# Scores of 64-feature heads taken over half of the partitions, with even and odd heads in two PSUM banks

## The chip, the core and the metric

The kernel runs on one core of one Trainium2 chip. The metric is the device time of one execution in microseconds (us). Before the change the median of three runs is 1797.05 us (1796.57 to 1798.23). In the profile, PE is TensorE's multiplying part and PEld its loading of weights (the stationary operand), DVE is VectorE, ACT ScalarE, POOL GpSimd, and SP the engine that issues most DMAs.

## The reference, cut to what matters

Two blocks work on one sequence of 256 tokens with 1024 features. The first block has two layers, each with three branches, and two of them are attention with heads of 64 features; the second block has a sparse attention of 8 heads of 64 features, whose keys are chosen by an index score of 4 heads of 64 features.

```python
# first block, forgetting branch ("c"): 16 heads, per block of 128 queries
sc = jnp.einsum('bqhd,bkhd->bhqk', q[:, start:end], k[:, :end]) * scale
sc = sc + cum[:, :, start:end, None] - cum[:, :, None, :end]
probs = jax.nn.softmax(jnp.where(causal, sc, -inf), axis=-1)
# first block, sliding window branch ("b"): 16 query heads on 4 key heads, with a sink
scores = jnp.einsum('bnqkgd,bnskd->bnkgqs', qb, kb) * (HEAD_DIM ** -0.5)
probs = softmax(concatenate([where(mask, scores, -inf), sink]))[..., :-1]
# second block, sparse attention: index scores of 4 heads, then 8 heads over the chosen keys
sc = jnp.einsum('bqhd,bsd->bqhs', qib, kif) * (IDX_DIM ** -0.5)
iscore = jnp.einsum('bqh,bqhs->bqs', wib, relu(sc))
s = jnp.einsum('bqhd,bqkd->bqhk', qb, ks) * (DSA_HEAD_DIM ** -0.5)
```

The second block ends in a mixture of 32 experts (MoE), whose weights are most of what the kernel reads.

## The kernel before

**Layout.** Queries and keys are kept with features along the 128 partitions, so two heads of 64 features share a tile: the even head in partitions 0 to 63, the odd one in 64 to 127. A product of one head must leave the other out. The kernel before keeps the keys twice for that: `kz[c][0]` has the even heads' keys and zeros in the lower half, `kz[c][1]` the odd heads' keys and zeros in the upper half (lines 463, 464, 471 to 474 in branch c; 616 to 618, 636, 637 in branch b; 1131, 1132, 1140 to 1142 in the second block). So each score product runs over all 128 partitions, and the zeros cancel the other head.

**One group of heads** (`attn_heads`, line 337): the scores of 4 heads (128 keys) or 2 heads (256 keys) go into one PSUM bank `sc`, of which there are two; then DVE takes the maximum (349), ACT the exponentials with their sums (356), PE turns them round (365), ACT copies them out (367) and PE multiplies with the values into `pv` (370). In branch c every head has two products into the bank: queries by keys in float32, and a row of the decay sums `negsel_r` by `Rs` in float32r over all partitions (496). In branch b there is only the first, with one mask product for the whole bank. In the sparse attention (`dsa`) each head has its own mask product (1216).

**A float32 product** is recorded as two matmuls with a weight load each; a float32r product as one.

**Order of work.** Steps are written in a list per layer, and a scheduler orders the instructions of each engine when the kernel is built; between the steps of attention it puts the products of projections (`proj`), which are most of PE's work. PE takes its instructions in that order. The experts at the end (lines 1550, 1572) use weights of 64 columns for two experts side by side, one in columns 0 to 63 of the array, one in columns 64 to 127; the experts' other products use the full array.

The lines in question, of branch c:

```python
def scores(h, o, first):
    mm(o, qc[g][:, h // 2, t * 128:t * 128 + 128], kz[g][h % 2][:, h // 2, :nS], first, False)
    mm(o, negsel_r[:, 32 + 8 * g + h:33 + 8 * g + h].to_broadcast([128, 128]), Rs[:, :nS], False, False)
```

## Time and profile before

| what | value |
|---|---|
| median of the runs | 1797.05 us |
| the profiled execution | 1801.36 us, its span 1799.6 us |
| PE busy | 1688.6 us (94%) |
| DVE busy | 1025.9 us (57%) |
| ACT busy | 708.2 us (39%) |
| POOL busy | 318.4 us (18%) |
| chain that ended last | PE 70%, DMA 13%, DVE 11% |

The profiled execution took 4.3 us more than the median; 1.8 us of it lie outside the span. The two layers of the first block run until about 960 us, the second block's mixing until about 1320 us, and the experts to the end. A matmul's record lasts longer than the array is taken by it, since matmuls are pipelined: what a matmul costs in a dense row of them is the distance from its start to the next one's start.

### The profile page before, as it was taken

The numbers are of one execution on the slowest core, as the hardware profiler recorded it, in microseconds if no ns is written. First come the engines' busy times: TensorE is split into PE (matmuls) and PEld (weight loads), VectorE is DVE, ScalarE is ACT, GpSimd is POOL, SyncE is SP. The second block draws the span as 40 slices with busy tenths as digits, with TensorE's granted clock in tenths as the row PEclk, the third lists the DMA queues.
The fourth block names the chain that finished last, engine by engine and source line by source line (L and its number), as shares of the span: only waits on it lengthen the run. The fifth ranks groups of instructions, "written<-read, shape, count | busy, mean of one in ns | idle before, by whom it ended". The sixth has DMA issues, their size and how long they took to land.

```text
span 1799.6 us, 24178 instructions
## 1 busy us (share of the span) xinstructions
PE 1688.6 (94%) x9005; PEld 1266.1 (70%) x9005; DVE 1025.9 (57%) x1659; ACT 708.2 (39%) x1345; POOL 318.4 (18%) x247
## 2 busy tenths in 40 slices
PE   7999999999999999999998998876879999999998
PEld 6899888888798999888877876765644444434342
DVE  6656656666673568675669899799631212212121
ACT  4455555644444656565546552421411010100000
POOL 0111106220102101321024343365100000000000
PEclk9999999999999999999999998987989999999999
DMA  8654445455566534453664633223699999999997
GB/s 261 188 142 137 140 145 144 148 166 164 164 174 178 171 111 141 135 164 102 197 190 149 180 106 111 66 70 107 196 378 369 410 409 408 409 409 409 409 409 297
DMA packets 186104, 389.65 MB, mean 217 GB/s; under 512 B 28736, under 2 KB 66816, under 8 KB 185984
## 3 DMA queue, kind: packets, MB, share of 16 engines
q1 hardware_dynamic: 185984, 388.08, 63.3%
q8 instruction: 72, 1.18, 0.3%
q14 instruction: 48, 0.39, 0.1%
HBM read 386.98 MB, written 1.05 MB: 216 GB/s over the span
## 4 chain that ended last, share of the span: by engine, by line
PE 70%; DMA 13%; DVE 11%; issue 2%; POOL 2%; ACT 1%; SPq 0%; DVEq 0%; POOLq 0%; ACTq 0%
PE proj L149 45%; PE proj L1550 7%; PE sc L149 5%; PE pv L149 4%; PE sc L1572 4%; DMA whi<-in_w_up_dram 2%; DMA Tlo<-in_w_up_dram 2%; DVE wlo L217 2%; PE tp L1509 1%; PE tp L365 1%; PE tp L286 1%; DMA wlo<-in_w_up_dram 1%; DMA wx<-in_w_up_dram 1%; DMA wraw<-in_w_down_dram 1%; DVE u L935 1%
## 5 line engine op out<-in xcount | busy, mean ns | idle before, releaser
L216 ACT CAST whi<-wraw 128x1024 fp32r<-128x1024 f32 x336 | 351.8, 1051 | 319.0 <-PE proj L149 263.1
L217 DVE TENSOR_TENSOR wlo<-wraw,whi 128x1024 fp32r<-128x1024 f32 (+1 forms) x287 | 376.7, 1316 | 172.0 <-PE proj L149 119.2
L149 PE MATMUL proj<-wlo,Thi 128*128 128x512 f32 (+1 forms) x1056 | 419.4, 397 | 6.2 <-DVE wlo L217 6.2
L149 PE MATMUL proj<-whi,Thi 128*128 128x512 f32 (+1 forms) x1056 | 419.4, 399 | 2.3 <-ACT P L988 1.0
L149 PE MATMUL proj<-whi,Tlo 128*128 128x512 f32 (+1 forms) x1056 | 415.7, 396 | 2.4 <-DVE Tlo L288 2.4
L149 PEld LDWEIGHTS proj<-wlo,Thi 128*128 128x128 f32 x1056 | 201.3, 191 | 48.3 <-DVE wlo L217 8.0
L149 PEld LDWEIGHTS proj<-whi,Thi 128*128 128x128 f32 x1056 | 201.4, 191 | 44.6 <-DVE u L1273 1.9
L149 PEld LDWEIGHTS proj<-whi,Tlo 128*128 128x128 f32 x1056 | 200.9, 190 | 43.1 <-DVE Tlo L288 2.9
L217 POOL TENSOR_TENSOR wlo<-wraw,whi 128x1024 fp32r<-128x1024 f32 (+1 forms) x49 | 125.4, 2559 | 434.4 <-PE proj L149 332.4
L149 PE MATMUL proj<-Thi,whi 128*128 128x256 f32 x576 | 165.2, 291 | 6.0 <-DVE u L468 3.0
L149 PE MATMUL proj<-Thi,wlo 128*128 128x256 f32 x576 | 165.8, 289 | 3.6 <-DVE wlo L217 3.6
L149 PE MATMUL proj<-Tlo,whi 128*128 128x256 f32 x576 | 164.8, 290 | 0.1
L1554 DVE SCALAR_TENSOR_TENSOR th<-th,cg,proj 128x512 f32<-128x512 f32 x16 | 12.0, 747 | 214.1 <-PE proj L1550 212.0
L149 PEld LDWEIGHTS proj<-Thi,whi 128*128 128x128 f32 x576 | 112.5, 197 | 7.8 <-DVE u L468 3.2
L149 PEld LDWEIGHTS proj<-Thi,wlo 128*128 128x128 f32 x576 | 113.5, 197 | 4.0 <-DVE wlo L217 3.8
L149 PEld LDWEIGHTS proj<-Tlo,whi 128*128 128x128 f32 x576 | 112.6, 197 | 0.4 <-DVE Tlo L959 0.3
L149 PE MATMUL sc<-u 128*128 128x256 f32 (+1 forms) x416 | 101.0, 359 | 11.8 <-DVE u L930 11.8
L1553 ACT ACTIVATE th<-proj,cg 128x512 f32<-128x512 f32 x16 | 11.0, 687 | 192.4 <-PE proj L1550 192.4
L149 PEld LDWEIGHTS sc<-u 128*128 128x128 f32 x416 | 70.6, 198 | 20.0 <-issue 11.9
L1576 DVE TENSOR_TENSOR u<-sc,u 128x512 fp32r<-128x512 f32 x32 | 22.0, 692 | 109.5 <-ACT u L1575 90.4
L356 ACT ACTIVATE P<-sc,nm 128x256 f32<-128x256 f32 (+1 forms) x152 | 63.7, 432 | 36.2 <-DVE nm L349 22.1
L1575 ACT CAST u<-sc 128x512 fp32r<-128x512 f32 x32 | 18.6, 585 | 136.1 <-PE sc L1572 122.0
(464 smaller groups left out, 2489.1 us busy)
## 6 DMA issues: line engine op xcount, KB each, us to landing
wraw<-in_w_in_dram SPq DMA_DIRECT2D x236, 512.0 KB, 3.8
wraw<-in_w_proj_dram SPq DMA_DIRECT2D x48, 512.0 KB, 4.3
u<-in_w_up_dram SPq DMA_DIRECT2D x25, 512.0 KB, 10.2
wraw<-in_w_out_dram SPq DMA_DIRECT2D x24, 512.0 KB, 4.4
u<-in_w_gate_dram SPq DMA_DIRECT2D x24, 512.0 KB, 10.2
wraw<-in_w_up_dram SPq DMA_DIRECT2D x21, 512.0 KB, 10.2
whi<-in_w_down_dram SPq DMA_DIRECT2D x21, 512.0 KB, 10.2
u<-in_w_down_dram SPq DMA_DIRECT2D x21, 512.0 KB, 10.1
```

What stands on the lines that cost most here:

```text
L149: T.matmul(o, l, r, start=start, stop=stop)
L216: S.copy(hi[:, :, :n], raw[:, :, :n])
L217: (G if share[0] and scount[0] % share[0] == 0 else V).tensor_sub(lo[:, :, :n], raw[:, :, :n], hi[:, :, :n].bitcast(F32))
L286: T.transpose(ps[:, b, :], src[:, b * 128:(b + 1) * 128], ident)
L356: S.activation(P[:, i * nS:(i + 1) * nS], scv[:, i, :], AF.Exp, bias=nm[:, i:i + 1], accum_out=l_out[:, i:i + 1])
L365: T.transpose(tp[:, j, :], P[:, j * 128:(j + 1) * 128], ident)
L935: V.tensor_tensor_scan(m[:, 256:512], rb, hi, 0.0, op0=OP.mult, op1=OP.add)
L1509: pin(T.matmul(tp[:, k, :], src[t][:, k0 + k, :], ohv[:, t], start=n == 0, stop=n == 3))
L1550: pin(T.matmul(ps[r], xk, w[:, 512 * j:512 * j + 512], start=k == 0, stop=k == 7))
L1572: pin(T.matmul(po[c][r], hT[:, k, r], w[:, 512 * c:512 * c + 512], start=k == 0, stop=k == 3))
L1575: S.copy(yh[:, c], po[c])
L1576: V.tensor_sub(yl[:, c], po[c], yh[:, c].bitcast(F32))
```

## The change

A score product now takes only the 64 partitions of its head, of the queries and of the keys (`half_of`). Keys are kept once, so the second tile, its zeros (POOL) and one of the two copies (DVE) fall away, and ACT's copy covers all 128 partitions. `attn_heads` takes two groups of heads at once, the even heads and the odd heads, each with a bank `sc` of its own; the products alternate between the two, and what follows runs for the even group first and then the odd one. In `dsa` the mask product is one for each bank; the index scores (`select`) put even and odd heads in two banks as well. The memory branch calls with one group and computes as before. In branch c the product with `negsel_r` still follows each head's product.

```diff
-        sc = psum.tile([128, 512], F32, name="sc", bufs=2)
-        scv = sc[:, :nh * nS].rearrange("p (h s) -> p h s", h=nh)
-        for i, h in enumerate(heads):
-            scores(h, scv[:, i, :], i == 0)
-        if masks is not None:
-            masks(scv)
...
+        sc = [psum.tile([128, 512], F32, name="sc", bufs=2) for _ in groups]
+        scv = [v[:, :nh * nS].rearrange("p (h s) -> p h s", h=nh) for v in sc]
+        for i in range(nh):
+            for v, h in zip(scv, hs):
+                scores(h[i], v[:, i, :], i == 0)
+        for v, g, heads in zip(scv, groups, hs):
+            if masks is not None:
+                masks(v)
...
+    def by_halves(nh):
+        return [[slice(h0 + j, h0 + 2 * nh, 2) for j in range(2)] for h0 in range(0, 8, 2 * nh)]
+    def half_of(h):
+        return slice(64 * (h % 2), 64 * (h % 2) + 64)
...
-                S.copy(kz[c][0][0:64, b, :], ps[0:64, :])
-                V.tensor_copy(kz[c][1][64:128, b, :], ps[64:128, :])
...
-            for j in range(2):
-                G.memset(kz[c][j][64 * (1 - j):64 * (1 - j) + 64], 0.0)
-            proj_fm(xT, W, OFF1["ck"] + 512 * c, 512, ev_k(c))
+            k = kz[c] = unit().rearrange("p (h s) -> p h s", h=4)
+            proj_fm(xT, W, OFF1["ck"] + 512 * c, 512, lambda b, ps: S.copy(k[:, b, :], ps))
...
-                mm(o, qc[g][:, h // 2, t * 128:t * 128 + 128], kz[g][h % 2][:, h // 2, :nS], first, False)
+                p = half_of(h)
+                mm(o, qc[g][p, h // 2, t * 128:t * 128 + 128], kz[g][p, h // 2, :nS], first, False)
                 mm(o, negsel_r[:, 32 + 8 * g + h:33 + 8 * g + h].to_broadcast([128, 128]), Rs[:, :nS], False, False)
...
-            S.copy(Q["kT"][0][0:64, :, tt], tp[0:64])
-            V.tensor_copy(Q["kT"][1][64:128, :, tt], tp[64:128])
+            S.copy(Q["kT"][:, :, tt], tp)
...
-                mm(o, qT[g][:, h // 2, t * 128:t * 128 + 128], kT[h % 2][:, 2 * g + h // 4, :nS], first, False)
+                p = half_of(h)
+                mm(o, qT[g][p, h // 2, t * 128:t * 128 + 128], kT[p, 2 * g + h // 4, :nS], first, False)
...
-            G.memset(kT, 0.0)
...
-                for j in range(2):
-                    V.tensor_copy(kT[0:64, 2 * j, tt], tp[0:64, 2 + j, :])
-                    V.tensor_copy(kT[64:128, 2 * j + 1, tt], tp[64:128, 2 + j, :])
+                V.tensor_copy(kT[:, 0:2, tt], tp[:, 2:4, :])
...
+            ps = [psum.tile([128, 512], F32, name="sc", bufs=2) for _ in range(2)]
             for p in range(2):
...
+                    mm(ps[a][:, 256 * p:256 * p + 256], iT[half_of(a), p, t * 128:t * 128 + 128],
+                       kT[half_of(a), 1, :], True, True)
...
-                mm(o, qT[:, h // 2, t * 128:t * 128 + 128], kT[:, h % 2, :], True, False)
-                mm(o, ident_r, selm[t], False, True)
+                mm(o, qT[half_of(h), h // 2, t * 128:t * 128 + 128], kT[half_of(h), 0, :], first, False)
+            def masks(o):
+                mm(o, ident_r, selm[t][:, None, :].to_broadcast([128, 2, 256]), False, True)
```

Since the scheduler orders anew, three places on PE show what stands in a row. A name is the bank written, then what streams through the array and what is loaded as weights; numbers tell buffers apart.

PE in branch c, layer 0, the first block of queries, before: in bank `sc_1169` and then `sc_1197`, products of odd heads (keys `u_817`) and even heads (`u_816`) with the decay product between them.

```order
L149 MATMUL sc_1169<-u_817,u_687 128x128
L149 MATMUL sc_1169<-Rs_229,negsel_r_87 128x128
L149 MATMUL sc_1169<-mask_r_89,ident_r_85 128x512
L149 MATMUL sc_1197<-u_816,u_687 128x128
L149 MATMUL sc_1197<-Rs_229,negsel_r_87 128x128
L149 MATMUL sc_1197<-u_817,u_687 128x128
```

The same place in the changed kernel, where `sc_1155` takes even heads and `sc_1156` odd ones.

```order
L149 MATMUL proj_1088<-Tlo_98,whi_1121 128x256
L149 MATMUL sc_1155<-u_816,u_687 128x128
L149 MATMUL sc_1155<-Rs_229,negsel_r_87 128x128
L149 MATMUL sc_1156<-u_816,u_687 128x128
L149 MATMUL sc_1156<-Rs_229,negsel_r_87 128x128
```

Between any two products over half of the partitions stands a product over all of them; all 64 score products of branch c in the two layers stand alone like this, or have a full product of another kind beside them.

PE in branch b, layer 0, the first block of queries, before: four heads in one bank, the mask, and the next bank.

```order
L149 MATMUL sc_3057<-u_2774,u_2773 128x128
L149 MATMUL sc_3057<-u_2775,u_2773 128x128
L149 MATMUL sc_3057<-mask_r_89,ident_r_85 128x512
L149 MATMUL sc_3086<-u_2774,u_2773 128x128
L149 MATMUL sc_3086<-u_2775,u_2773 128x128
```

The same place in the changed kernel: the last two of eight products that alternate between the halves, and then both masks.

```order
L149 MATMUL sc_3038<-u_2760,u_2759 128x128
L149 MATMUL sc_3039<-u_2760,u_2759 128x128
L149 MATMUL sc_3038<-mask_r_89,ident_r_85 128x512
L149 MATMUL sc_3039<-mask_r_89,ident_r_85 128x512
L149 MATMUL proj_3293<-whi_3271,Thi_95 128x512
```

Here eight half products stand in a row, even and odd by turns, ahead of the masks of both banks.

PE in the sparse attention of the second block, before: two heads of one bank, each with its mask.

```order
L149 MATMUL proj_10809<-whi_10804,Thi_9153 128x512
L149 MATMUL proj_10809<-wlo_10805,Thi_9153 128x512
L149 MATMUL sc_10594<-u_9586,u_9938 128x256
L149 MATMUL sc_10594<-selm_9936,ident_r_85 128x256
L149 MATMUL sc_10594<-u_9586,u_9938 128x256
```

The same place in the changed kernel: two even heads together, one mask, and projections again; the odd heads' bank follows 23 rows later.

```order
L149 MATMUL proj_10755<-whi_10751,Tlo_9116 128x512
L149 MATMUL sc_10549<-u_9548,u_9893 128x256 x2
L149 MATMUL sc_10549<-selm_9891,ident_r_85 128x512
L149 MATMUL proj_10756<-whi_10751,Thi_9115 128x512
L149 MATMUL proj_10756<-wlo_10752,Thi_9115 128x512
```

The scheduler has parted the two banks here, so that two products of the same half stand together and none of the other half beside them.

## Rows read from the trace of the kernel before

**Rows 1.** Head of the page: span; chain that ended last, by engine.
```profile
span 1799.6 us, 24178 instructions
...
PE 70%; DMA 13%; DVE 11%; issue 2%; POOL 2%; ACT 1%; SPq 0%; DVEq 0%; POOLq 0%; ACTq 0%
```

**Rows 2.** Windows: stretch, length, busy time by engine, PEclk granted, DMA share, GB/s.
```profile
100.00:200.00 100.00, 100.00 (x722) 94.32 (x721) 66.20 (x99) 60.83 (x128) 13.77 (x11) 1.00 0.48 135
300.00:400.00 100.00, 100.00 (x527) 85.60 (x526) 67.41 (x115) 58.68 (x138) 26.16 (x18) 1.00 0.50 152
600.00:700.00 100.00, 100.00 (x672) 91.78 (x671) 67.51 (x107) 59.37 (x125) 2.57 (x3) 1.00 0.49 140
...
1100.00:1240.00 140.00, 112.29 (x493) 91.28 (x492) 127.00 (x181) 39.10 (x78) 71.05 (x53) 0.85 0.22 69
```

**Rows 3.** Timeline of PE in branch c: start, length, instruction (two stretches).
```profile
118.54 0.44 PE L149 MATMUL sc<-u 128*128 128x128 f32 x2
...
118.87 0.44 PE L149 MATMUL sc<-u 128*128 128x128 f32 x2
...
200.63 0.59 PE L149 MATMUL sc<-u 128*128 128x256 f32 x2
...
201.18 0.28 PE L149 MATMUL sc<-mask_r,ident_r 128*128 128x256 f32 x1
```

**Rows 4.** Timeline of PE in branch b: banks of four heads, and of two.
```profile
305.86 1.05 PE L149 MATMUL sc<-u 128*128 128x128 f32 x8
...
306.99 1.05 PE L149 MATMUL sc<-u 128*128 128x128 f32 x8
...
343.73 1.03 PE L149 MATMUL sc<-u 128*128 128x256 f32 x4
...
344.83 0.40 PE L149 MATMUL proj<-whi,Thi 128*128 128x512 f32 x1
```

**Rows 5.** Timeline of PE in the experts: full array, then weights of 64 columns.
```profile
1381.78 0.63 PE L1509 MATMUL tp<-oh,u 128*128 128x256 f32 x4
...
1382.34 0.64 PE L1572 MATMUL sc<-we,hT 128*64 128x512 f32 x1
...
1382.35 0.64 PE L1572 MATMUL sc<-u,hT 128*64 128x512 f32 x1
...
1382.82 0.59 PE L1572 MATMUL sc<-we,hT 128*64 128x512 f32 x1
...
1383.25 0.59 PE L1572 MATMUL sc<-we,hT 128*64 128x512 f32 x1
```

**Rows 6.** Timeline of PE and PEld in the experts: 64 columns, then full array.
```profile
1455.34 0.59 PE L1550 MATMUL proj<-we,u 128*64 128x512 f32 x1
...
1455.86 0.19 PEld L1586 LDWEIGHTS pv<-u,ohT 128*128 128x128 f32 x1 [0.81 <-issue]
1455.87 0.50 PE L1586 MATMUL pv<-u,ohT 128*128 128x512 f32 x1
...
1456.20 0.39 PE L1587 MATMUL pv<-u,ohT 128*128 128x512 f32 x1
...
1456.43 0.40 PE L1586 MATMUL pv<-u,ohT 128*128 128x512 f32 x1
```

**Rows 7.** By source line: copies and zeros of the keys; shortest, median, longest in ns.
```profile
L464 DVE COPY u<-proj x16: 427/428/429, 87.7 to 554.5; 64x256 f32<-64x256 f32 x16
L637 DVE COPY u<-tp x4: 694/694/695, 299.0 to 777.9; 64x512 f32<-64x512 f32 x4
L473 POOL MEMSET u<- x8: 944/946/952, 74.2 to 491.6; 64x1024 f32 x8
L618 POOL MEMSET u<- x4: 944/948/950, 256.5 to 728.6; 64x1024 f32 x4
```

**Rows 8.** Waits of PE: who waited for whom, us in total, times, longest.
```profile
PE pv L149 <- ACT PT L367: 0.9, 1, 0.9
```

**Rows 9.** Costliest groups of the page: the exponentials of all heads.
```profile
L356 ACT ACTIVATE P<-sc,nm 128x256 f32<-128x256 f32 (+1 forms) x152 | 63.7, 432 | 36.2 <-DVE nm L349 22.1
```

More of the change, by code (lines that the diff above doesn't have):

```diff
@@ L334, in run_steps, with attn_heads @@
             steps[name](*(int(v) for v in arg))
[L337 removed]
+    def attn_heads(groups, scores, vsrc, pv, pcol, nS, lsum, sink=None, masks=None):
         nb = nS // 128
[L341 to L370 removed]
@@ new lines, in attn_heads @@
+        hs = [list(range(g.start, g.stop, g.step or 1)) for g in groups]
+        nh = len(hs[0])
+        sc = [psum.tile([128, 512], F32, name="sc", bufs=2) for _ in groups]
[6 more added lines that the diff above has]
+                masks(v)
+            nm = wtile([128, 8], F32, name="nm", bufs=4)
+            V.tensor_reduce(nm[:, :nh], v, axis=AX.X, op=OP.max, negate=True)
+            if sink is not None:
+                ns, sk = (k[:, g] for k in sink)
+                V.tensor_tensor(nm[:, :nh], nm[:, :nh], ns, op=OP.min)
+                V.tensor_tensor(nm[:, 4:4 + nh], nm[:, :nh], sk, op=OP.add)
+            P = wtile([128, 512], F32, name="P", bufs=2)
+            for i, h in enumerate(heads):
+                S.activation(P[:, i * nS:(i + 1) * nS], v[:, i, :], AF.Exp, bias=nm[:, i:i + 1],
+                             accum_out=lsum[:, h:h + 1])
+            if sink is not None:
+                es = wtile([128, 4], F32, name="es", bufs=4)
+                S.activation(es[:, :nh], nm[:, 4:4 + nh], AF.Exp)
+                V.tensor_tensor(lsum[:, g], lsum[:, g], es[:, :nh], op=OP.add)
+            tp = psum.tile([128, 4, 128], F32, name="tp", bufs=2)
+            n = nh * nb
+            for j in range(n):
+                T.transpose(tp[:, j, :], P[:, j * 128:(j + 1) * 128], ident)
+            PT = wtile([128, 4, 128], F32, name="PT", bufs=2)
+            S.copy(PT[:, :n, :], tp[:, :n, :])
+            for i, h in enumerate(heads):
+                for b in range(nb):
+                    mm(pv[:, pcol(h)], PT[:, i * nb + b, :], vsrc(h, b), b == 0, b == nb - 1)
@@ L1214, in scores @@
             def scores(h, o, first):
[L1215 to L1220 removed]
+                mm(o, qT[half_of(h), h // 2, t * 128:t * 128 + 128], kT[half_of(h), 0, :], first, False)
+            def masks(o):
+                mm(o, ident_r, selm[t][:, None, :].to_broadcast([128, 2, 256]), False, True)
+            for groups in by_halves(2):
+                attn_heads(groups, scores, lambda h, b: vd[:, b, :], pv,
+                           lambda h: slice(h * 64, h * 64 + 64), 256, lsum, masks=masks)
             head_norm(yd, pv, lsum, 1.0)
```

78 lines of the change are left out of this document (21 added, 57 removed).

## The prediction

> **What bounds the kernel now.** I read the head of the page first, then the busy time by stretch, then single products in the timeline. The chain that ended last is 70% PE [rows 1]. In the stretches in which the two attention branches of the first block run, PE is busy all the time at the full clock (granted 1.00, the 2.4 GHz level), while DVE is busy 58 to 68% and ACT 52 to 61% of it [rows 2]. So in the first block a microsecond more or less on PE is a microsecond more or less of the kernel, and work taken from DVE, ACT or POOL gives nothing. The experts at the end stream their weights once the second block has left its buffers, so that a delay before them moves them as a whole; I see nothing there that gives it back. In the second block's sparse attention PE is busy 112 of 140 us and DVE 127 of 140 us at a granted clock of 0.85 [rows 2]: there DVE sets the end, and PE time counts in part.
>
> **What a score product costs now.** In branch c, a head with 128 keys takes 0.33 us from its first matmul to the next head's (118.54 to 118.87), a head with 256 keys 0.55 us (200.63 to 201.18) [rows 3]. In branch b a bank of four heads takes 1.13 us from start to start (305.86 to 306.99), a bank of two heads 1.10 us (343.73 to 344.83) [rows 4]; a 512-column mask or projection product takes 0.23 us of that (1456.20 to 1456.43 for one of the same width) [rows 6]. What is left is 0.90 and 0.87 us, so a float32 product takes 0.22 us at 128 keys (8 matmuls, 0.11 each) and 0.43 us at 256 keys (4 matmuls, 0.22 each).
>
> **What running two halves at once can save.** The trace has no product over half of the partitions, but it has its sister: the experts' products over half of the columns. Two of them, one for each half, start 0.01 us apart (1382.34 and 1382.35) and the next two 0.43 us after that (1382.82 to 1383.25) [rows 5]. A float32 matmul of 256 columns takes 0.22 us, so one of 512 alone would take 0.43 us: the two run in the time of one. I take the same for row halves, where products of both halves stand beside each other. That they do must be read from the new order of PE, and there it is so only in places. I counted all 152 half products in that order; they stand in 94 runs that a full-array product ends:
> - Branch c: 64 runs of a single product, since the decay product over all partitions stands behind each. Nothing to overlap: saving 0.
> - Branch b: 19 runs. Three of eight by turns save four products each, and two of three save one: 14 products at 128 keys, 14 x 0.22 = 3.1 us. Three runs of four save two each, two of two one each, two of three one each: 10 at 256 keys, 10 x 0.43 = 4.3 us. The rest are two products of the same half or single ones, which save nothing. Sum 7.4 us.
> - Index scores and sparse attention: 11 runs, of which only one of four has both halves: 2 x 0.43 = 0.9 us; the others are pairs of one half.
>
> In all 8.3 us at most.
>
> **What changing between half and full array costs.** This term is not in the change's intention, and it decides. Again the experts show it for columns. On the way in, four full products start at 1381.78 at about 0.12 us each (0.63 us with the last one's tail), so the next one was due at 1382.26; the first half product starts at 1382.34, 0.08 late, and the first pair takes 0.48 us to the second where the next takes 0.43, 0.05 more [rows 5]. On the way out, the last pair starts at 1455.34 and its place ends 0.43 us later, at 1455.77; the next weight load starts at 1455.86, only 0.07 us before the last half product's record ends, 0.09 late; and from the first full product to the second it is 0.33 us (1455.87 to 1456.20) where the next takes 0.23, 0.10 more [rows 6]. So at each change the array runs empty and then waits for weights that could otherwise load behind a product. A round trip costs 0.08 + 0.05 + 0.09 + 0.10 = 0.32 us; with the rounding of these starts I take 0.33.
>
> The Trainium skill has this as a rule that speaks against the change: "TensorEngine Tiling (Array Packing)", section Key Properties, says that changing the tiling mode, not just the tile, drains the engine. For column halves the trace agrees (the load that waits until 0.07 us before the end); for row halves no run here shows it yet. By the rule the sum below holds; without it rival 1 holds.
>
> For row halves the price is bounded by 0 from below (a change of form gives no reason for a gain) and by 0.40 us from above: the 0.05 on the way in is for 64 columns of weights, the 0.10 on the way out for 128 columns; a row half has 128 columns, so 0.08 + 0.10 + 0.09 + 0.10 = 0.37, with rounding 0.40. I take 0.33, the price of the nearest rows.
> - Branch c: 64 x 0.33 = 21.1 us, all on the path, since PE is 100% busy there [rows 2].
> - Branch b: 19 x 0.33 = 6.3 us against 7.4 us saved: -1.1 us.
> - Second block: 11 x 0.33 = 3.6 us less 0.9 saved = 2.7 us; PE has slack there and DVE ends last, so I count half, 1.4 us.
>
> **What is removed beside PE.** DVE loses 16 copies of 0.43 us and 4 of 0.69 us, POOL 12 zero fills of 0.95 us [rows 7]; ACT's copies keep their number and their free size. That is 9.6 us of DVE and 11.4 us of POOL, and 0 on the path: PE's products hide it, as DVE is busy about two thirds there. If that cover were gone (DVE last), it would give back up to 9.6 us. The few copies and the one zero fill less in the second block are smaller, and I leave them out. The mask products of the sparse attention are half as many and twice as wide: 0.
>
> **The two banks.** Both are now taken by one pair of groups, so the next pair's odd products wait until ACT has read the odd bank, and PE's queue waits behind them: the transposes, `pv` products and projections that follow. PE waited 0.9 us in all for ACT's `PT` before [rows 8], and the scheduler puts projections between. I take 0 and carry the other end as rival 3.
>
> **Sum.** 21.1 - 1.1 + 1.4 = +21.4 us. The profiled execution, 1801.36 us with a span of 1799.6, would become 1822.8. It lay 4.3 us over the median of the runs, so against the median 1797.05 + 21.4 = 1818.4, say 1818 us.
>
> **Rivals.**
> 1. Row halves change without running empty, because the full array's columns and their way to PSUM stay as they are. Then only the saving is left: 1797 - 8.3 = 1789 us, faster. For it: the rows show the price for columns alone. Against it: the load that waits for the end [rows 6] looks like a property of any change of form. It decides if the round trip is below 8.3 / 94 = 0.09 us.
> 2. Half the price: the array runs empty (0.08 + 0.09 = 0.17 us) but weights load ahead. 94 x 0.17 = 16.0 less 8.3: 1805 us.
> 3. The banks: PE stands still while ACT reads the odd bank. Of the 152 exponentials at 0.43 us [rows 9], 8 belong to the memory branch and half of the rest, 72, to odd groups: 72 x 0.43 = 31 us if PE had nothing else in its queue, some 15 us if it had in half of the places. It decides where no projection stands between two pairs. On top of the forecast that is 1834 us. Against it: PE's wait for ACT was 0.9 us [rows 8].
> 4. The change does nothing of what it says: halves neither overlap nor cost. Then 1797 us.
>
> **How the numbers follow.** Forecast with the price from 0.25 to 0.40 us (94 x 0.40 - 8.3 = 29, so up to 1826): 0.62. Rival 2: 0.12. Rival 1: 0.15. Rival 3: 0.06. Rival 4: 0.05. The likeliest gives 1818 us. The range must leave out no more than 2 in 10: from 1796 (it takes in rivals 2 and 4) to 1830 (the upper bound and a little of rival 3); rival 1 and most of rival 3 are left out. A change by over 0.2%, 3.6 us, is about what a measurement of this kernel can tell from none. Faster is rival 1, with the tail of others: 0.16. Same is rival 4 and the thin place between rivals 1 and 2: 0.07. Slower is the rest: 0.77.
>
> **What would show it.** In the changed kernel's timeline a head of branch c should take about 0.66 us at 128 keys and 0.9 us at 256 keys, where it took 0.33 and 0.55. The first weight load behind a half product should begin only when that product's record is nearly over. In the run of eight in branch b, an even and an odd product should start about 0.01 us apart, and the eight should take about 0.9 us. The start of the second block should come some 20 us later, and the experts' stretch should have the same length. I am wrong if a head in branch c takes 0.33 and 0.55 us as before, or if PE gets idle time with ACT as its releaser in the attention stretches.

## The result, and the profile after

The changed kernel takes 1841.24 us (median of four runs, 1838.12 to 1845.59), the kernel before 1797.12 us (now four runs as well): ratio 1.0248, 95% interval 1.0228 to 1.0269, or 44 us slower. The forecast was slower, but by 21 us (1818 us), and its range ended at 1830. The profiled execution took 1838.12 us with a span of 1836.3 us; its span is 36.7 us longer than that of [rows 1].

First the head of the page of the changed kernel, and the same stretches as in [rows 2] (stretch, length, busy time by engine, granted clock, DMA share, GB/s):

```profile
span 1836.3 us, 24106 instructions
...
PE 68%; DMA 14%; DVE 10%; issue 3%; POOL 2%; ACT 1%; SPq 0%; DVEq 0%; ACTq 0%; POOLq 0%
```

```profile
100.00:200.00 100.00, 98.73 (x611) 87.10 (x610) 49.43 (x77) 46.39 (x105) 5.74 (x6) 0.88 0.40 115
300.00:400.00 100.00, 99.44 (x543) 82.56 (x542) 64.97 (x98) 57.59 (x139) 40.90 (x35) 1.00 0.49 145
600.00:700.00 100.00, 100.00 (x593) 84.79 (x592) 51.18 (x77) 50.53 (x111) 7.47 (x5) 0.97 0.42 121
1100.00:1240.00 140.00, 122.53 (x567) 96.37 (x565) 124.13 (x184) 49.14 (x96) 63.86 (x48) 0.91 0.25 76
```

In the first block PE is nearly as busy as in [rows 2] (98.7 to 100 of 100 us), but gets less done: 611 matmuls from 100 to 200 us where 722 had started before. And the granted clock, 1.00 in the first block before, is 0.88 and 0.97 in the two stretches in which branch c runs. In branch b's stretch it is 1.00 still.

The timeline of PE in branch c of the changed kernel, first at 128 keys, then at 256, with the weight loads (PEld) of the first head; start, length, instruction, as in [rows 3]:

```profile
113.51 0.49 PE L149 MATMUL sc<-u 64*128 64x128 f32 x2
113.93 0.33 PE L149 MATMUL sc<-Rs,negsel_r 128*128 128x128 f32 x1
114.18 0.48 PE L149 MATMUL sc<-u 64*128 64x128 f32 x2
...
117.58 0.79 PE L149 MATMUL sc<-u 64*128 64x128 f32 x2
118.31 0.47 PE L149 MATMUL sc<-Rs,negsel_r 128*128 128x128 f32 x1
118.71 0.79 PE L149 MATMUL sc<-u 64*128 64x128 f32 x2
...
217.40 0.70 PE L149 MATMUL sc<-u 64*128 64x256 f32 x2
...
218.33 0.70 PE L149 MATMUL sc<-u 64*128 64x256 f32 x2
```

```profile
113.51 0.29 PEld L149 LDWEIGHTS sc<-u 64*128 64x128 f32 x2
113.93 0.18 PEld L149 LDWEIGHTS sc<-Rs,negsel_r 128*128 128x128 f32 x1
```

A head takes 0.67 us at 128 keys (113.51 to 114.18) and 0.93 at 256 (217.40 to 218.33); it took 0.33 and 0.55 [rows 3]. The decay product's weights begin to load at 113.93, 0.07 us before the half product's record ends at 114.00, as the experts' rows had it for columns [rows 6]. At 117.58 the same head takes 1.13 us (to 118.71): the granted clock has just gone from 1.00 to 0.50, from the 2.4 GHz level to the 1.2 GHz one:

```profile
113.50:117.00 3.50, 3.50 (x17) 2.53 (x17) 1.23 (x1) 1.32 (x2) 0.00 (x0) 1.00 0.70 195
117.40:124.20 6.80, 6.80 (x26) 5.92 (x27) 1.29 (x2) 2.90 (x16) 0.00 (x0) 0.50 0.06 24
```

Branch b's run of eight, and at 256 keys two products of the same half beside a run of four by turns:

```profile
327.43 0.39 PE L149 MATMUL proj<-whi,Tlo 128*128 128x512 f32 x1
327.74 1.16 PE L149 MATMUL sc<-u 64*128 64x128 f32 x16
328.83 0.73 PE L149 MATMUL sc<-mask_r,ident_r 128*128 128x512 f32 x2
329.41 0.40 PE L149 MATMUL proj<-whi,Thi 128*128 128x512 f32 x1
...
365.91 1.13 PE L149 MATMUL sc<-u 64*128 64x256 f32 x4
366.97 0.50 PE L149 MATMUL sc<-mask_r,ident_r 128*128 128x512 f32 x1
...
373.63 1.14 PE L149 MATMUL sc<-u 64*128 64x256 f32 x8
374.70 0.50 PE L149 MATMUL sc<-mask_r,ident_r 128*128 128x512 f32 x1
```

The overlap is there: at 256 keys four products by turns (x8, two matmuls each) take 1.07 us, no longer than two of the same half (x4, 1.06 us). Eight products at 128 keys take 1.09 us (327.74 to 328.83) where two banks took 0.90 each [rows 4]; their matmuls start in pairs 0.007 us apart (327.743 and 327.750 us for the first two).

How much of the 44 us branch c has is read from stretches that hold the same work. From a projection matmul ahead of branch c to one behind it (the 601st and the 1081st matmul into `proj` in the first layer, the 2641st and the 3241st in the second), first before, then after:

```profile
111.26:220.34 109.08, 109.08 (x765) 101.78 (x764) 71.21 (x108) 64.69 (x146) 10.44 (x4) 1.00 0.47 133
591.76:740.33 148.57, 148.57 (x987) 135.79 (x986) 99.74 (x148) 89.24 (x193) 15.52 (x10) 1.00 0.46 132
```

```profile
107.66:242.18 134.52, 133.25 (x769) 113.50 (x767) 70.45 (x105) 65.01 (x146) 10.41 (x4) 0.90 0.38 108
614.32:778.37 164.05, 163.81 (x990) 140.70 (x989) 97.45 (x149) 89.01 (x193) 12.20 (x8) 0.98 0.42 119
```

Nearly the same number of matmuls (765 and 769, 987 and 990), 25.4 and 15.5 us longer: 40.9 us, which is 4.2 more than the span's 36.7. Most of the 4.2 is a spell at the lower clock that the profiled execution before had ahead of branch c and this one had not: branch c began at 111.26 us there, at 107.66 here. The experts' first product starts 37.7 us later (1326.07 before, 1363.72 after) and the span is 36.7 us longer: the length of the experts' stretch is unchanged to 1 us.

### The profile page after: what moved, and what is told of

It reads as the page before. It is cut to its first block, busy times and chain, and to the rows that moved or that the text cites. A ratio compares the mean times of both kernels' runs of the same rounds, so it can differ in the third digit from the quotient of the medians.

```text
span 1836.3 us, 24106 instructions
## 1 busy us (share of the span) xinstructions
PE 1726.4 (94%) x8997; PEld 1267.8 (69%) x8997; DVE 1008.9 (55%) x1633; ACT 708.0 (39%) x1345; POOL 302.9 (16%) x234
## 4 chain that ended last, share of the span: by engine, by line
PE 68%; DMA 14%; DVE 10%; issue 3%; POOL 2%; ACT 1%; SPq 0%; DVEq 0%; ACTq 0%; POOLq 0%
PE proj L149 42%; PE proj L1552 6%; PE sc L149 6%; PE pv L149 4%; PE sc L1574 3%; DMA Tlo<-in_w_up_dram 2%; DMA wx<-in_w_up_dram 2%; DMA whi<-in_w_up_dram 2%; DVE wlo L217 2%; PE tp L369 2%; PE tp L286 1%; PE tp L1511 1%; DMA u<-in_w_down_dram 1%; DMA wlo<-in_w_up_dram 1%; DMA wraw<-in_w_down_dram 1%
## 5 line engine op out<-in xcount | busy, mean ns | idle before, releaser
L149 PE MATMUL sc<-u 64*128 64x256 f32 (+3 forms) x416 | 103.5, 389 | 10.5 <-DVE u L932 10.2
L149 PEld LDWEIGHTS sc<-u 64*128 64x128 f32 (+1 forms) x416 | 61.4, 197 | 31.7 <-issue 17.5
L353 DVE TENSOR_REDUCE nm<-sc 128x2 f32<-128x512 f32 (+1 forms) x60 | 39.6, 686 | 64.3 <-PE sc L149 64.3
```

Source lines behind the costliest of these rows:

```text
L149: T.matmul(o, l, r, start=start, stop=stop)
L353: V.tensor_reduce(nm[:, :nh], v, axis=AX.X, op=OP.max, negate=True)
```

## The experiments

Theory A: each change between half and whole array costs some 0.33 us, branch c pays it 64 times, and the lower granted clock comes with it. The rivals are named where they are tested. Each kernel differs from the changed kernel or from one named, and was timed beside the kernel before on the same chip (1795.3 to 1796.5 us).

### Which part carries the loss

e1_c_full, branch c undone:

```
-                p = half_of(h)
-                mm(o, qc[g][p, h // 2, ...], kz[g][p, h // 2, :nS], first, False)
+                mm(o, qc[g][:, h // 2, ...], kz[g][h % 2][:, h // 2, :nS], first, False)
...
-            for groups in by_halves(nh):
+            for groups in ([slice(h0, h0 + nh)] for h0 in range(0, 8, nh)):
```

> The changed kernel with branch c as it was before: keys twice with zeros, products over the whole array, one bank at a time. Branch b, the index scores and the sparse attention keep their products over half of the rows (30 runs of them instead of 94). Theory A, the loss is branch c's 64 changes of form (0.34 us each, a head of 128 keys takes 0.67 us instead of 0.33) and the lower granted clock that came with them: what is left is -1.1 us from b and +1.4 us from the second block, so 1797 us, between 1793 and 1801, granted clock 1.00 from 100 to 300 us. Rival B, the pairing of two banks or the second block carries a good part of the +44 us: 1805 us or more.

Measured: 1804.53 us, ratio 1.0043 (1.0026 to 1.0060), granted clock 1.00 from 100 to 300 us. 37 us of the 44 went with branch c. What was left, +8 us, is more than the +0.3 expected.

e1_c_banks, the same with `by_halves` kept (pairs of banks, whole-array products):

```
-            for groups in ([slice(h0, h0 + nh)] for h0 in range(0, 8, nh)):
+            for groups in by_halves(nh):
```

> As e1_c_full, but branch c also takes its heads in pairs of banks, even and odd by turns, as the changed kernel does; all its products are over the whole array. Theory A: as e1_c_full within 2 us, 1795 to 1801 us. Rival B, the two banks make PE wait for ACT: some 15 to 31 us more than e1_c_full, 1812 us or more, with PE idle behind ACT's exponentials in the first block.

Measured: 1806.00 us, ratio 1.0058 (1.0041 to 1.0075): 1.5 us over e1_c_full, the intervals overlap. The two banks cost next to nothing; rival 3 of the prediction falls.

e2_b_only: e1_c_full with the second block as before (the same edit in `select`):

```
-                mm(o, qT[half_of(h), h // 2, ...], kT[half_of(h), 0, :], first, False)
+                mm(o, qT[:, h // 2, ...], kT[:, h % 2, :], True, False)
+                mm(o, ident_r, selm[t], False, True)
```

> e1_c_full with the index scores and the sparse attention also as they were before, so that only branch b uses half products (19 runs of them). e1_c_full lay 8 us over the kernel before, where the forecast's terms for b and the second block gave +0.3. Theory F, the second block's 11 runs cost it (its term was -1.4 us too kind by some 7): 1797 us, 1794 to 1799. Rival G, branch b costs it (19 changes of form against too small a saving): 1803 us or more.

Measured: 1795.35 us, ratio 0.9992 (0.9981 to 1.0003). Branch b is within the measurement of nothing, a little below, as forecast.

e3_second_only, e3_c_only and e4_no_second: the kernel before with the second block alone changed, with branch c alone changed, and the changed kernel with the second block as before. Beside the edits shown, the first two take branch b back:

```
-                mm(o, qT[g][p, h // 2, ...], kT[p, 2 * g + h // 4, :nS], first, False)
+                mm(o, qT[g][:, h // 2, ...], kT[h % 2][:, 2 * g + h // 4, :nS], first, False)
```

> The kernel before with only the index scores and the sparse attention changed (11 runs of half products). By difference they cost 1804.5 - 1795.4 = 9.2 us. Theory F: 1796.5 + 9 = 1805 us, between 1801 and 1809; 11 x 0.33 - 0.9 = 2.7 us of it are changes of form, the rest a lower granted clock between 1130 and 1170 us, where PE is busy without a break: 0.75 or less over 1140 to 1160 us, where the kernel with b alone had 1.00. Rival I: the loss belongs to branch b and the second block together: under 1800 us.

> The kernel before with branch c alone changed as in the changed kernel (64 lone half products, two banks). Difference of the runs so far: 1841.2 - 1804.5 = 36.7 us for c. Theory A: 64 x 0.33 = 20.8 us for the changes of form and some 16 us for the lower granted clock: 1833 us, between 1829 and 1837, granted clock under 0.93 from 100 to 200 us. Rival: branch b or the second block take part in what c costs (the clock falls because of all of them together): under 1826 us.

> The changed kernel with the index scores and the sparse attention as they were before; branches b and c as changed. If the parts add up: 1841.2 - 7.7 = 1833.5 us, between 1830 and 1837. If the second block's loss does not come on top of branch c's (c alone gave 1843.0, b alone -1.2): 1842 us, between 1838 and 1845, and then its 11 changes of form cost nothing in the changed kernel, and all of the +44 us is branch c's.

Measured: the second block alone 1803.59 us, 1.0049 (1.0030 to 1.0068), +7.7 us. Branch c alone 1843.03 us, 1.0272 (1.0248 to 1.0295), over its expectation: as much as the whole change. The change without the second block 1839.90 us, 1.0245 (1.0230 to 1.0261). So the parts do not add up: the second block costs some 8 us where branch c is not changed, and about nothing where it is (1.3 us by the two medians, -0.4 us by the distance of each from its own runs of the kernel before). Two stretches of the same length show where the second block pays; first the kernel with the second block alone, then the one with b alone, both from 1140 us, then the changed kernel, 36 us later:

```profile
1140.00:1160.00 20.00, 20.00 (x89) 16.51 (x88) 5.72 (x10) 8.01 (x19) 1.34 (x1) 0.69 0.03 3
```

```profile
1140.00:1160.00 20.00, 20.00 (x128) 18.02 (x128) 12.35 (x15) 12.26 (x27) 7.35 (x5) 1.00 0.26 79
```

```profile
1176.00:1196.00 20.00, 20.00 (x98) 16.09 (x98) 6.33 (x12) 8.95 (x25) 0.00 (x0) 0.76 0.00 1
```

In these 20 us PE is busy without a break and DVE 6 to 12 us: here PE sets the end, and the granted clock decides, 0.69 against 1.00. The whole place has two ends that every kernel shares, the 4536th and the 4537th matmul into `proj`, with the sparse attention between them. For the kernel before, the second block alone, the changed kernel and e4_no_second:

```profile
1130.59:1155.44 24.85, 22.38 (x137) 19.48 (x135) 13.73 (x32) 12.92 (x40) 4.90 (x5) 0.86 0.00 1
```

```profile
1123.36:1155.74 32.38, 30.08 (x132) 23.88 (x130) 14.59 (x35) 13.03 (x40) 4.88 (x5) 0.68 0.00 1
```

```profile
1165.90:1193.56 27.66, 25.35 (x131) 19.64 (x130) 14.60 (x35) 13.04 (x40) 4.89 (x5) 0.81 0.00 1
```

```profile
1170.08:1192.22 22.14, 19.52 (x136) 16.99 (x135) 13.88 (x34) 12.94 (x40) 4.95 (x5) 1.00 0.00 1
```

All twelve traces with the 11 changes have 27.7 to 32.4 us here, the six without them 22.0 to 24.9; length times granted clock is 20.8 to 22.6 us in all eighteen. So nearly all of the difference is the clock, and the changes lower it here too: the place takes 5.5 us more in the changed kernel than in e4_no_second, and 7.5 us more with the second block alone than in the kernel before. But e4_no_second comes to this place 4.2 us behind the changed kernel (39.5 us behind the trace before, against 35.3), leaves it 1.3 us ahead, and loses 3 us again behind it. Why, the runs don't settle: the second block's other low spells lie differently in each kernel.

### The price of a change of form, without half scores

e1_half_decay_only: e1_c_full, with the decay product over 64 rows; `Rc` holds both parts of the decay rows in each half.

```
-                mm(o, negsel_r[:, 32 + 8 * g + h:...].to_broadcast([128, 128]), Rs[:, :nS], False, False)
+                mm(o, negsel_r[0:64, 8 * g + h:...].to_broadcast([64, 128]), Rc[0:64, :nS], False, False)
```

> As e1_c_full (branch c's score products over the whole array, one bank at a time), but the decay product behind each head now runs over half of the rows (rows 0 to 63, from a copy of the decay rows that holds both parts there; four small copies per layer are added). So c has 64 changes of form and back, as in the changed kernel, but nothing runs beside anything, and the float32 products are full. Theory A, the price is one of the change of form itself: 64 x 0.34 = 21.8 us over e1_c_full, 1819 us, if the granted clock stays at 1.00; 1830 to 1842 us if it falls as in the changed kernel, and then the changes of form alone make it fall. Rival D, the price belongs to float32 half products (two weights each): under 1805 us. Rival C (low clock from half products of scores): 1819 us with the clock at 1.00.

Measured: 1831.33 us, ratio 1.0198 (1.0174 to 1.0221). The timeline of PE at 128 keys, and the two stretches of branch c:

```profile
116.88 0.49 PE L149 MATMUL sc<-u 128*128 128x128 f32 x2
117.30 0.32 PE L149 MATMUL sc<-Rc,negsel_r 64*128 64x128 f32 x1
117.55 0.49 PE L149 MATMUL sc<-u 128*128 128x128 f32 x2
```

```profile
108.31:228.63 120.32, 120.32 (x766) 103.53 (x765) 71.69 (x108) 65.23 (x146) 10.43 (x4) 1.00 0.39 121
600.16:759.90 159.74, 159.74 (x987) 137.79 (x986) 100.03 (x149) 89.51 (x193) 13.63 (x8) 1.00 0.39 122
```

A head takes 0.67 us again (116.88 to 117.55), though it is now the other product that is half: the price belongs to the change, not to float32 half products (rival D falls). At a granted clock of 1.00 the two stretches are 11.2 and 11.2 us longer than before: 22.4 us for 64 changes, 0.35 us each. This is the term of the forecast, 21.1 us, measured alone. (The run lies 27 us over e1_c_full by the medians, 24 by the spans of the two profiled executions; its expectation of 1819 us had counted e1_c_full as 1797.) What the changed kernel loses above it in branch c is 40.9 - 22.4 = 18.5 us. Its two stretches above split that: 0.10 x 134.5 + 0.02 x 164.1 = 17 us is the part of the clock that was not granted, and in 1.5 us PE is idle (busy 133.25 of 134.52 and 163.81 of 164.05), 1.3 us of it in one wait for ACT's exponentials.

### What lowers the clock

e1_c_grouped: all half products of a pair of banks first, then its decay products (22 runs instead of 64).

```
         for i in range(nh):
             for v, h in zip(scv, hs):
                 scores(h[i], v[:, i, :], i == 0)
+        if decays is not None:
+            for i in range(nh):
+                for v, h in zip(scv, hs):
+                    decays(h[i], v[:, i, :])
```

> The changed kernel, but in branch c all the half products of a pair of banks stand first and all its decay products behind them: 22 runs of half products in c instead of 64, and 19 of its 32 pairs beside each other. Theory A: price 22 x 0.34 = 7.5 us, saved 10 x 0.22 + 9 x 0.43 = 6.1 us, so c costs 1.4 us and the kernel takes about 1798 us (1794 to 1804), with a granted clock of 0.97 or more from 100 to 300 us. Rival C, the clock falls because products over half of the rows use less of the array, however they are ordered: the low stretches stay, granted clock under 0.92 from 100 to 200 us, and 1808 us or more.

Measured: 1806.71 us, ratio 1.0064 (1.0047 to 1.0081); granted clock 1.00 in both stretches, which take 113.3 and 149.8 us, 5.4 us over those before. The expectation counted the +8 us of the second block as nothing; against e1_c_full branch c costs 2.2 us, where 1.4 was worked out. Half products that stand together cost little and keep the clock here: rival C, as it was stated for these 64 half products, falls.

e2_all_half: the decay product over the head's own half (28 runs in c). e2_two_changes: e1_half_decay_only with two changes of form per head, all score products over the whole array. First the line of e2_all_half, then those of e2_two_changes behind the score product:

```
+                mm(o, negsel_r[p, 8 * g + h:...].to_broadcast([64, 128]), Rc[p, :nS], False, False)
...
+                mm(o, negsel_r[0:64, ...], Rc[0:64, :nS], False, False)
+                mm(o[:, nS - 128:], ident_r, causal_r, False, False)
+                mm(o, negsel_r[0:64, ...], Rc[0:64, :nS], False, ...)  
```

> The changed kernel, but the decay product of each head runs over the same half of the rows as its score product (even heads rows 0 to 63, odd heads rows 64 to 127 of a copy of the decay rows; four small copies per layer are added). Nothing of branch c but its masks is over the whole array: 28 runs of half products in c instead of 64. Theory A, changes of form and what comes with them: price 28 x 0.33 = 9.2 us against some 8 to 11 us saved, so within 3 us of e1_c_full's 1804.5 us, with a granted clock of 0.97 or more from 100 to 300 us. Rival C, half products lower the clock by themselves: there are twice as many of them now, so granted clock under 0.92 from 100 to 200 us and 1815 us or more.

> As e1_half_decay_only (score products over the whole array), but each head of branch c now has two changes of form: score product (whole array), decay product over half of the rows, mask product of the head (whole array, 128 columns), and the same decay product again, each of the two with half of its weight: 128 runs in c. Price by theory A at the full clock: 1831 + 64 x 0.33 + 64 small products of 0.05 to 0.11 us = 1856 us, between 1851 and 1861. Theory E, the array's standing still at the changes lowers the clock: it stands still for more of the time than in the changed kernel, so the granted clock from 100 to 200 us is 0.92 or less and the kernel takes 1866 us or more. Theory H, it takes lone score products over half of the rows as well: clock 0.97 or more there, about 1856 us.

Measured: e2_all_half 1813.08 us, ratio 1.0087 (1.0064 to 1.0110), 8.5 us over e1_c_full where 3 at most was expected; its first stretch of c has a granted clock of 0.94 and takes 118.70 us, its second 1.00 and 148.97. From 100 to 200 us the clock is 0.93, a little over rival C's bound of 0.92, from 100 to 300 us 0.97, theory A's bound: with twice as many half products the clock fell somewhat although there are only 28 runs, and rival C is not ruled out for these. The first of its two low spells begins at 125.7 us, behind a run of heads that transposes over the whole array cut into pieces. e2_two_changes 1887.19 us, ratio 1.0495 (1.0477 to 1.0512), with these stretches:

```profile
108.86:262.98 154.12, 154.12 (x842) 128.36 (x840) 73.34 (x110) 65.85 (x147) 10.43 (x4) 0.88 0.32 94
633.09:821.25 188.16, 188.16 (x1039) 157.83 (x1038) 99.00 (x149) 89.55 (x193) 12.47 (x8) 0.92 0.36 104
```

No score product is half here, and the clock falls further than in the changed kernel (0.88 and 0.92), so half score products are not needed for it. The number of half products has doubled along with the changes, to 128; e2_all_half has 128 as well, in 28 runs, and lost far less. So more changes lower the clock further, but their number alone does not decide: it fell in e2_all_half with 28 and did not in e1_half_decay_only with 64. The price at a full clock was put at 1856 us; the other 31 us agree with the clock that was not granted in the two stretches, 0.12 x 154.1 + 0.08 x 188.2 = 34 us.

That leaves why e1_half_decay_only kept its clock with the same 64 changes and the same 0.67 us per head. Its score products use all rows (half of them zeros), those of the changed kernel use 64. So the array does less between the changes there. Three runs, which test whether that is the reason, put work back.

e3_more_work and e4_eight_decays: three and eight decay products per head, with their weights divided, instead of one (the second kernel's edit):

```
-        S.mul(negsel_r, sel_r.bitcast(F32), -1.0)
+        S.mul(negsel_r, sel_r.bitcast(F32), -0.125)
...
+                for _ in range(8):
+                    mm(o, negsel_r[:, 32 + 8 * g + h:...].to_broadcast([128, 128]), Rs[:, :nS], False, False)
```

> The changed kernel with two more decay products behind each head of branch c: three of them over the whole array, with half, a quarter and a quarter of the weight. The changes of form stay (63 runs in c), and PE has 64 x 2 x 0.08 = 10.6 us more to do at the full clock. Theory E, the clock falls because the array does too little between the changes: it stays up or nearly so (granted clock of 0.96 or more from 100 to 200 us), some 16 us come back, and the kernel takes 1836 us, between 1830 and 1844, though it does more. Rival H, half products next to whole ones lower the clock whatever lies between: 1841 + 11 to 15 = 1852 us or more.

> The changed kernel with eight decay products behind each head of branch c, each over the whole array with an eighth of the weight; the 64 lone half products stay. An added decay product took 0.11 us in e3_more_work (0.894 us for a head of 128 keys with two more, against 0.671; 1.17 against 0.94 at 256 keys), so seven take 64 x 7 x 0.113 = 50.6 us at the full clock. Theory E, too little work in the array between the changes: granted clock 0.97 or more from 100 to 260 us, 16 to 20 us come back, 1841 + 51 - 18 = 1874 us, between 1866 and 1882. Rival H, half score products beside whole-array ones lower it whatever lies between: clock as in the changed kernel, 1841 + 51 + 5 to 15 = 1897 us or more.

Measured: 1860.14 us, 1.0363 (1.0340 to 1.0386), and 1895.18 us, 1.0562 (1.0542 to 1.0582): both as if the clock had not come back. The trace of the kernel with eight splits this by place, first around the first layer's branch c, then by the two stretches of branch c:

```profile
100.00:180.00 80.00, 80.00 (x534) 73.50 (x533) 29.62 (x46) 28.56 (x73) 3.36 (x5) 0.87 0.27 77
180.00:260.00 80.00, 80.00 (x497) 68.56 (x497) 42.57 (x61) 37.54 (x76) 7.58 (x3) 1.00 0.41 122
```

```profile
107.57:262.46 154.89, 154.89 (x984) 136.85 (x983) 70.98 (x105) 63.74 (x144) 9.99 (x4) 0.93 0.32 91
635.17:823.62 188.45, 188.45 (x1172) 164.96 (x1171) 95.53 (x145) 85.66 (x183) 11.23 (x8) 0.95 0.37 107
```

The 128-key heads of the first layer run from 113 to 150 us, in the first stretch, where the clock is low as ever; from 180 to 260 us, with 256 keys only, it is 1.00, where the changed kernel had 0.98 (one spell of 3.4 us). In the second layer it is 0.95, lower than the changed kernel's 0.98. Over branch c as a whole the time at the 1.2 GHz level, twice the share that was not granted, is 37.5 us in both kernels with added decay products and 34.1 in the changed one: this work did not bring the clock back. An added product of 128 columns takes 0.11 us, as in [rows 3] (0.22 us for two passes), twice what its columns need at the rate of the long products (512 columns take 0.23 us), so it adds less work than time.

e5_dense puts one product of 512 columns (identity times zeros) behind each head of 128 keys; e5_dense_base is the same kernel without it, the masks ahead of the heads in both.

```
+                if fill is not None:
+                    fill(v, i == nh - 1)
...
+            def fill(o, last):
+                mm(o, ident_r, zero_r[:, None, :].to_broadcast([128, nh, nS]), False, last)
```

> The changed kernel, but at 128 keys branch c's mask products stand ahead of the heads of a pair of banks instead of behind them (the base for e5_dense; no work added). As the changed kernel: 1841 us, between 1836 and 1847, and low granted clock behind the 128-key heads as there (24 us of it in all, of 34 us in branch c).

> e5_dense_base with one product more behind each 128-key head of branch c: the identity times zeros, over the whole array and 512 columns (0.23 us at the full clock), added to the head's bank, so that the result is the same. 32 x 0.23 = 7.4 us of work more; the 64 changes of form stay. Theory E, the idle share of the array lowers the clock: the low stretches behind the 128-key heads go (under 7 us of low clock there instead of 24), some 10 us come back, and it takes 1841 + 7 - 10 = 1838 us, no longer than e5_dense_base or less. Rival H, half score products beside whole-array ones lower it whatever lies between: the low stretches stay, 1849 us or more.

Measured: 1842.19 us, 1.0254 (1.0233 to 1.0275), without the added products, and 1833.48 us, 1.0211 (1.0191 to 1.0231), with them. The kernel that does 7.4 us more is 8.7 us faster, and the mean granted clock of each of its three runs (0.971 to 0.975) lies over each of the base's (0.965 to 0.967). But where? The stretches of branch c, base first:

```profile
107.63:235.91 128.28, 128.28 (x766) 110.33 (x765) 70.79 (x105) 64.73 (x146) 10.45 (x4) 0.93 0.38 113
611.99:773.58 161.59, 161.59 (x975) 138.30 (x974) 96.14 (x147) 86.24 (x185) 12.26 (x8) 0.98 0.43 124
```

```profile
107.78:238.56 130.78, 130.78 (x783) 109.78 (x781) 69.99 (x105) 64.77 (x146) 10.43 (x4) 0.95 0.38 111
612.15:775.59 163.44, 163.44 (x996) 138.66 (x995) 96.63 (x147) 88.83 (x192) 12.18 (x8) 1.00 0.42 121
```

In the second layer the low spell is gone (0.98 to 1.00), and the stretch adds up at the full clock: 148.6 + 11.2 for the changes + 3.7 for the added products = 163.5. In the first layer a spell of 10 us behind the first run of heads and one of 3 us at 217 us are left (17 us at the lower level in the base), so the expectation (under 7 us) is missed. The two stretches got 4.4 us longer for 7.4 us of work: 3 us of clock came back in branch c, not 10. The gain of the whole lies behind it: from the sparse attention to the experts the profiled execution with the added products is 11.6 us shorter. The other eleven kernels with the 11 changes take 189.7 to 199.0 us for the same work, this one 186.2, so that the added products are the cause is not shown.

What is shown: the clock falls in branch c in all kernels with 63 to 128 runs of half products there, but for one, and in e2_all_half with 28; it keeps its level in every kernel without half products there and in the three with 14 to 22 runs (e1_c_grouped and the two versions below). The exception, e1_half_decay_only, fits the thought that the work between the changes counts, and so does the second layer of e5_dense; e3_more_work and e4_eight_decays, in which the clock did not come back, speak against it. What in a run of changes lowers the clock, and why the first run of heads stays low, is open.

### A version that beats both

Half products pay where they stand together. e2_halves_kept: all of branch c's products but the masks over halves, the runs of b and c held in order (18 and 17 runs), the second block as before. e3_opened: a whole-array product opens both banks ahead of the run, so that it starts only when both are free (14 and 12 runs).

```
+        if opens is not None:
+            for v, h in zip(scv, hs):
+                chain(opens(h[0], v[:, 0, :]))
         for i in range(nh):
             for j in range(len(groups)):
...
+                chain(scores(hs[j][i], scv[j][:, i, :], ...))
```

> Branch c as in e2_all_half, with the half products of a pair of banks held together in their order (even and odd by turns, decay products behind them), the same for branch b, and the second block as it was before. Runs of half products: 18 in c, 17 in b. Theory A: c pays 18 x 0.33 = 5.9 us and saves 16 x 0.33 + 16 x 0.55 = 14.1 us, less some 2 us where a run is cut in two: -6.2 us. b pays 17 x 0.4 = 6.8 us and saves 16 x 0.22 + 16 x 0.43 = 10.4 us less 2: -1.6 us. Sum 1796.2 - 7.8 = 1788 us, between 1784 and 1793. Rival B, holding runs together makes PE wait for both banks: 1797 us or more.

> e2_halves_kept with the runs kept whole: in branch b the mask products open the two banks, in branch c at 256 keys a whole-array decay product of the first head opens each bank, so that a run starts only when both banks are free. 14 runs in c and 12 in b instead of 18 and 17. Theory A: 9 x 0.35 = 3.2 us of changes less and 8 pairs more beside each other, 8 x 0.43 = 3.4 us: 1792.6 - 6.6 = 1786 us, between 1781 and 1791. Rival B, waiting for both banks costs as much as it saves: 1792 us or more.

Measured: 1792.59 us, 0.9978 (0.9968 to 0.9987), and 1789.94 us, 0.9966 (0.9956 to 0.9975): 4 and 6 us faster than the kernel before, both within their expectations, near the upper ends. In the trace of the second, four heads of 256 keys with their decay products:

```profile
142.87 0.39 PE L149 MATMUL sc<-Rs,negsel_r 128*128 128x256 f32 x2
143.19 1.14 PE L149 MATMUL sc<-u 64*128 64x256 f32 x8
143.97 0.47 PE L149 MATMUL sc<-Rc,negsel_r 64*128 64x256 f32 x2
144.37 0.50 PE L149 MATMUL sc<-mask_r,ident_r 128*128 128x256 f32 x2
```

From 142.87 to 144.37 they take 1.50 us; four heads at 0.55 us took 2.2 [rows 3]. The granted clock is 1.00 in both stretches of branch c, which take 105.8 and 145.4 us against 109.1 and 148.6.

## Why the prediction was right in sign and wrong in size

- **What bounds the kernel**: right for the first block and the experts. (The lower ends of its shares of DVE and ACT, 58 and 52%, are those of 200 to 300 us, 58.92 and 51.82%, which [rows 2] does not show.) Wrong for one place: "there DVE sets the end" in the second block. The mean over 140 us hid 20 us in which PE is never idle and DVE mostly is.
- **What running two halves at once can save**: right. Pairs run in the time of one, and only where the order puts them side by side; no head of branch c did.
- **The price of a change of form**: right. 0.33 us was taken from the experts' column halves; a head showed 0.67 us (0.66 forecast) and 0.93 instead of 0.9, and 64 changes cost 22.4 us at the full clock instead of 21.1. In branch b, between products of 512 columns, a round trip is dearer: the eight take 1.09 us instead of 0.88, the product ahead of them 0.31 instead of 0.23, the two masks behind 0.58 instead of 0.46, 0.41 us together. The Trainium skill, "TensorEngine Tiling (Array Packing)", section Key Properties, has the rule behind this (a change of tiling mode drains the engine); the weight load that waits until 113.93 agrees with it for row halves too.
- **Branch b**: -1.1 us forecast, -1.2 us measured (interval -3.4 to +0.5). With the dearer round trip of 0.41 us the same sum gives 19 x 0.41 - 7.4 = +0.4 us, which the interval holds as well; that the two numbers agree so closely is luck.
- **Second block**: +1.4 us forecast. In the changed kernel it was 1.3 us by two medians whose intervals overlap, and -0.4 us by their distances from the kernel before; alone it was 7.7 us. The number held by luck: half was counted because DVE was thought to end last, and the loss that there is comes from the clock.
- **The two banks**: taken at 0, and measured next to nothing (1.5 us in e1_c_banks). The sign that was to prove the forecast wrong, PE idle with ACT as its releaser, came once, for 1.3 us.
- **The term that failed is one that the sum did not have.** All its prices were taken at a granted clock of 1.00, because the clock was 1.00 in the first block before [rows 2]. It did not stay there. In the profiled execution branch c lost some 17 us to it, 13 of them in the first layer; with the price of the changes, 22.4 us, and 1.5 us in which PE was idle, that is the 40.9 us of branch c. The upper bound of the range, 0.40 us for each change, was a bound on the wrong quantity: the prices hardly differed from the forecast, the speed at which everything else ran did. The trace before had the warning: in the second block, where PE stands still between pieces of work, its granted clock was 0.85 [rows 2]. A rival "the changes lower the clock", priced from that row, has branch c's 258 us at a granted clock between 0.85 and 1.00, so up to 258 x (1 / 0.85 - 1) = 45 us on top of the forecast; it would have put 1841 inside the range. That is a bound and no forecast: PE was idle for 28 of the 140 us in that row, and in branch c it hardly is.
- Of the rivals, none came true; rival 3 gave a near number (1834) for a reason that e1_c_banks rules out, but for the 1.3 us named above.
- **Bridge**: 44.1 us between medians is 36.7 between the two profiled spans, 4.2 by which the profiled execution before lay over its median, and 3.1 by which the one after lay under its own.

## What to carry to other kernels

Before products are moved to halves of the array, count in the built order how often form changes, and price each change at a third of a microsecond; pairs that do not stand side by side save nothing. A change that puts many changes of form into a stretch must also be priced at a lower clock, for all that runs in that stretch. And a mean over a stretch does not say which engine ends it: look for the pieces inside it in which one engine never rests.

## What the runs showed of the hardware that was not expected

- The granted clock fell to the 1.2 GHz level within the first run of lone half products (its first eight heads), although the records show PE busy without a break. The time at that level, twice the missing share of a stretch's clock, was 34 us in branch c of the changed kernel, 68 us with 128 changes and no half score product, none with 22 changes, but also none with 64 changes and whole score products, and 14 us with 28 changes and 128 half products. The Trainium skill, "TensorE: Matmul & The Clock Gate", section "A second HAM failure mode: psum-queue depth-cycling", tells of a kernel in which short standstills between groups of matmuls made the clock go to and fro. The trace of the changed kernel agrees in that the clock goes to and fro, with five low spells in branch c; that the changes of tiling are the standstills is not shown.
- A kernel with 32 more products of 512 columns (7.4 us of work) was 8.7 us faster. Branch c, where they were added, got 4.4 us longer; the gain came in a later block that was not touched, with a higher granted clock, and that the added products caused it is not shown.
- In the sparse attention eighteen kernels took 22.0 to 32.4 us for a place that is 20.8 to 22.6 us long when each time is multiplied by its granted clock.
- The losses of the parts do not add: +7.7 us (second block) and +47 us (branch c) alone, +44 us together.
